# Block sums in the feature stage, values and convolved input kept in high and low parts, and head loads by token halves

## The chip, the cores and the metric

One core of a Trainium2 chip runs the kernel. The metric is the device time in microseconds (us) of one execution, as the median of several runs. A profile of one execution by the hardware profiler stands beside the runs. The engines are named as in the profile: PE (TensorE matmuls) and PEld (its weight loads), DVE (VectorE), ACT (ScalarE), POOL (GpSimd) and SP (SyncE, whose queue issues every DMA of this kernel).

## What is computed

Two layers over 1024 latent tokens of width 1024, with 256 context tokens beside them in the first. The cut below leaves out norms, conditioning and the second layer (a pooling mixer on a grid).

```python
xm, z, og = split(h @ w_in, 3)                    # 3 x 2048 columns
xc = silu(short_conv(xm, conv_w, conv_b))
q, k = headwise(xc, w_q), headwise(xc, w_k)       # 4x4 blocks
v = headwise(xm, w_v)
gates = concat(q, k, v) @ w_gate + b_gate         # two directions
h_f, h_b = mlstm_scan(q, k, v, gates), its mirror # 4 heads of 512
y = sigmoid(og) * headnorm(h_f + h_b) + skip * xc
out = (y * silu(z)) @ w_out
```

The scan is computed by the kernel in its parallel form: for each head and each tile of 128 tokens, scores of the tile's queries against all 1280 tokens, times a matrix of decays, times the values.

## The kernel before, in words

Matmuls take f32r operands. To keep the precision of f32 every operand is split into a high part (a copy by ACT, rounded to f32r) and a low part (the rest, a subtraction by DVE), and a product is three matmuls (`mm3`, L144): high x high, high x low, low x high. All of them are issued at L133. The order of PE's instructions is written out by hand in the stages below; on the other engines the framework orders the work.

**Start (to about 83 us).** Conditioning, norms and `modulate` (L300): the normalized input h, eight tiles of 128 channels by 1024 tokens, in high and low parts that stay in SBUF.

**Feature stage (about 83 to 360 us).** A loop over 16 blocks n of 128 channels. `features(n)` (L342) multiplies a weight tile by h for three token chunks (512, 512, 256), copies the product out (L361 to L364), convolves it, stores the convolved input to `xc_d` (L371, L372) and splits it (L376 to L378). `token_part(n)` (L381) is a generator that runs beside the products of the next block, a step after every second k: for each of ten blocks of 128 tokens it multiplies by `vv` (a block-diagonal matrix for the values and 16 gate columns, in high and low parts) with two matmuls, of 288 and of 144 columns (L398, L399), adds the two halves by a reduction (L400) and collects the values in `vst`, which goes to `v_d` (L402). In passes 2 to 9 POOL adds the high and the low part of h again (L503) and the sum is stored to `h_d` for later.

**Products for z and the output gate (about 360 to 688 us).** The first pair of channel blocks is computed plainly (`plain`, L599), in 64 steps; the generators `gates` (L419: logs of the gates, transposes at L460, scans at L469 to L473, rows stored to `a_d` at L479) and `sums` (L513) are run at given steps of it. `sums(k)` loads two tiles of h from `h_d` (L516), forms four block sums on DVE (L520 to L523) and splits them (L526, L527) into the 16 tiles `T_`. The other seven pairs use Strassen's seven products (`strassen`, L534): sums of weights on POOL (L543 to L546), split at L553 and L554, and the tiles `T_`.

**Heads (about 688 to 1256 us).** Four heads of eight query tiles. A head loads its four tiles of convolved input and one of context (`fetch_x`, L655) and five of values (`fetch_v`, L668), each 512 KB, in f32, and splits them itself (`cast_low`, L649: ACT at L651, then POOL or, in the first head, DVE at L652). `make_A` and `make_q` (L692, L701) make the queries of two tiles at a time. For each tile: `decay` (L736) makes the decay matrix M from gate rows with ACT, and POOL masks the diagonal (L750, L751); `score_chunk` (L713) computes scores for three chunks and multiplies them into M on DVE (L731); `weights` (L753) normalizes M (L757 to L765). One tile later `turn` (L767) transposes M and splits it (L774, L775), and `values` (L778) multiplies by the values; two tiles later `store` (L799) transposes back, scales on DVE (L805), adds on POOL (L806) and stores. A fifth of the second layer's conditioning (`ada_part`, L633) runs on DVE beside the tiles, with weights loaded into `wr`.

**The rest (from about 1256 us)** is the output product, the second layer and its norms.

What orders the work around the change: PE's order by hand; the buffers of a tag (S4: 32 of 4 KB a partition, T5: 5, wr, wh and wl: 2 each, hn: 3, pt: 6; PSUM pa: 3, pb: 2, pc: 3), each free again when its last reader is done; and SP's one queue.

Of the kernel before, what the change touches and what calls it, by code (L numbers as in the profile page):

```python
# [17 lines left out]
P = 128  # L18
# [20 lines left out]
SUM_STEPS = (16, 24, 32, 40)  # L39
# [13 lines left out]
def hybrid_block(ctx: ExitStack, tc: tile.TileContext, xT, ctxT, vecs, w_ada0, w_ada, w_blk, w_krow, blk_mask, w_gate, w_in, b_gate, w_out,  # L53
# [68 lines left out]
    xc_d = dr.tile([KE, P, TA], F32, name="xc_d")  # L122
    v_d = dr.tile([NH, P, 10, DH], F32, name="v_d")
    h_d = dr.tile([KD, P, T], F32, name="h_d")
    y1_d = dr.tile([KE, P, T], F32, name="y1_d")
# [184 lines left out]
    for k in range(KD):  # L310
        if k < 4:
# [4 lines left out]
            modulate(x_sb[k], [(*h[k, hf], slice(512 * hf, 512 * hf + 512)) for hf in range(2)], k, 0)  # L316
        else:
# [3 lines left out]
            modulate(x_sb[k], [(*pair, slice(0, T))], k, 0)  # L321
# [20 lines left out]
    def features(n, side):  # L342
# [28 lines left out]
        nc.sync.dma_start(xc_d[n, :, 0:T], yl)  # L371
        nc.sync.dma_start(xc_d[n, :, T:TA], yc)  # L372
# [3 lines left out]
        for s_, h_, l_ in ((yl, xch[0], xcl[0]), (yc, xch[1], xcl[1])):  # L376
            S.activation(h_, s_, AF.Copy)
            V.tensor_tensor(l_, s_, f(h_), op=ALU.subtract)  # L378
        return xmh, xml, xch, xcl

    def token_part(n, xmh, xml, xch, xcl):  # L381
# [8 lines left out]
        vst = tl("T5", [P, 10, 144])  # L390
        for s in range(10):
            yield
            if s < 8:
                ah, al = xmh[0][:, s * P:(s + 1) * P], xml[0][:, s * P:(s + 1) * P]
            else:
                ah, al = xmh[1][:, (s - 8) * P:(s - 7) * P], xml[1][:, (s - 8) * P:(s - 7) * P]
# [95 lines left out]
    side, parts = iter(()), []  # L492
    with ctx0:
        for n in range(KE):
# [18 lines left out]
        def sums(k):  # L513
            t0, t1 = tl("T5", [P, T]), tl("T5", [P, T])
            for t, kk in ((t0, k), (t1, k + 4)):
                nc.sync.dma_start(t, h_d[kk])  # L516
            b11, b12, b21, b22 = t0[:, :512], t0[:, 512:], t1[:, :512], t1[:, 512:]
            for j in range(1, 5):
                T_[j, k] = tl("S4", [P, 2, 512], F32R)
            V.tensor_tensor(b22, b22, b12, op=ALU.subtract)  # L520
            V.tensor_tensor(b12, b12, b11, op=ALU.subtract)
            V.tensor_tensor(b11, b22, b11, op=ALU.add)
            V.tensor_tensor(b21, b21, b11, op=ALU.subtract)  # L523
            for j, x in ((2, b11), (3, b22), (1, b12), (4, b21)):
                t = T_[j, k]
                S.activation(t[:, 0], x, AF.Copy)  # L526
                V.tensor_tensor(t[:, 1], x, f(t[:, 0]), op=ALU.subtract)  # L527
# [716 lines left out]
```

## Time and profile before

| | |
|---|---|
| median of 3 runs | 2089.25 us (2087.11 to 2090.32) |
| the profiled execution's own time | 2086.98 us |
| its span, first to last instruction | 2085.2 us |
| mean granted clock of PE | 0.979 |
| PE busy | 1994.8 us (96%) |
| DVE busy | 1329.5 us (64%) |
| ACT busy | 772.6 us (37%) |
| POOL busy | 475.4 us (23%) |
| moved by DMA | 272.33 MB, mean 131 GB/s |

A row of the table by stage gives, for a stretch of the span, the busy time of each engine with its number of instructions, the granted clock of PE as a share of full speed, the mean busy share of the 16 DMA engines and what they moved. A row of a timeline begins with the start and the length in us; rows of equal instructions are merged (x3), and a bracket at the end is idle time of the engine before the row, with what ended it. A row of the waits reads: engine, tile and line that waited, <- who ended the wait, total us, times, longest. PE's matmuls overlap, so a row's length holds the latency of its last one; starts give the rate.

### The profile page before, as it was taken

How to read it: one execution, taken by the hardware profiler on the slowest of the kernel's cores; microseconds unless marked ns; L12 is line 12 of the kernel's file. 1: busy time of each engine (PE TensorE's matmuls, PEld its weight loads, DVE VectorE, ACT ScalarE, POOL GpSimd, SP SyncE). 2: the span in 40 equal slices, each digit the busy share in tenths (PEclk: the TensorE clock that was granted, in tenths of full speed). 3: DMA queues.
4: the chain of work that ended last, by engine and by line, in shares of the span. 5: the costliest groups of instructions: out<-in, count | busy, mean ns of one | idle time of the engine just before them, and what ended most of it. 6: DMA issues, size and time to landing. Idle time of an engine off the chain costs nothing.

```text
span 2085.2 us, 26407 instructions
## 1 busy us (share of the span) xinstructions
PE 1994.8 (96%) x10050; PEld 1674.5 (80%) x10050; DVE 1329.5 (64%) x2136; ACT 772.6 (37%) x1201; POOL 475.4 (23%) x482
## 2 busy tenths in 40 slices
PE   7899999799999899999999999999999999999998
PEld 5688888678888787778878888887888888888897
DVE  4877777877767868777677572354657273754444
ACT  5444444333334533333324232443423122224443
POOL 4411100032322313331333211252100000000275
PEclk9999999889999999999999999999999999999999
DMA  7233334444443636135234143434331212224473
GB/s 298 74 130 134 135 104 134 131 147 141 141 152 123 212 116 199 56 130 162 97 114 144 41 152 130 170 140 150 113 121 51 89 58 76 66 94 154 162 256 129
DMA packets 158335, 272.33 MB, mean 131 GB/s; under 512 B 10332, under 2 KB 89692, under 8 KB 158208
## 3 DMA queue, kind: packets, MB, share of 16 engines
q1 hardware_dynamic: 158208, 270.64, 39.1%
q8 instruction: 79, 1.29, 0.3%
q14 instruction: 48, 0.39, 0.1%
HBM read 205.41 MB, written 65.20 MB: 130 GB/s over the span
## 4 chain that ended last, share of the span: by engine, by line
PE 79%; DVE 12%; DMA 3%; issue 3%; POOL 2%; ACT 1%; SPq 0%; DVEq 0%; POOLq 0%; ACTq 0%
PE pa L133 40%; PE pc L133 31%; PE pb L133 6%; PE pb L772 1%; POOL S L961 1%; DMA wr<-in_w_ada_dram 1%; DVE S L306 1%; DVE wl L641 1%; DVE T L763 1%; DVE T L731 1%; POOL hn L941 1%; DVE T L765 1%; DVE S L304 1%; DVE den L759 1%; PE pc L803 1%
## 5 line engine op out<-in xcount | busy, mean ns | idle before, releaser
L133 PE MATMUL pa<-S,wh 128*128 128x512 f32 (+1 forms) x2496 | 723.5, 374 | 7.5 <-DVE S L306 7.2
L133 PEld LDWEIGHTS pa<-S,wh 128*128 128x128 f32 x2496 | 446.1, 190 | 81.3 <-DVE S L306 11.1
L133 PE MATMUL pc<-S,wh 128*128 128x512 f32 (+1 forms) x1616 | 454.9, 367 | 9.3 <-ACT wh L553 6.3
L133 PE MATMUL pa<-S,wl 128*128 128x512 f32 (+1 forms) x1248 | 460.6, 369 | 3.3 <-DVE wl L141 3.3
L133 PEld LDWEIGHTS pc<-S,wh 128*128 128x128 f32 x1616 | 294.6, 190 | 60.0 <-ACT wh L553 6.7
L141 DVE TENSOR_TENSOR wl<-wr,wh 128x1024 fp32r<-128x1024 f32 (+1 forms) x124 | 147.4, 1189 | 271.2 <-ACT wh L139 270.3
L133 PE MATMUL pc<-S,wl 128*128 128x512 f32 (+1 forms) x808 | 295.2, 367 | 3.9 <-DVE wl L554 2.9
L139 ACT ACTIVATE wh<-wr 128x1024 fp32r<-128x1024 f32 (+1 forms) x124 | 124.6, 1005 | 404.7 <-PE pa L133 183.4
L133 PEld LDWEIGHTS pa<-S,wl 128*128 128x128 f32 x1248 | 236.6, 190 | 44.2 <-DVE wl L141 3.7
L133 PE MATMUL pa<-S,S 128*128 128x512 f32 (+1 forms) x1152 | 251.1, 367 | 14.6 <-DVE T L731 14.6
L133 PE MATMUL pc<-S,pt 128*128 128x512 f32 x960 | 233.7, 397 | 0.0
L133 PEld LDWEIGHTS pa<-S,S 128*128 128x128 f32 x1152 | 195.7, 194 | 46.0 <-issue 11.6
L133 PEld LDWEIGHTS pc<-S,pt 128*128 128x128 f32 x960 | 179.5, 190 | 36.0
L133 PEld LDWEIGHTS pc<-S,wl 128*128 128x128 f32 x808 | 153.6, 190 | 29.9 <-DVE wl L554 3.6
L941 POOL TENSOR_TENSOR hn<-hn,pt 128x512 f32<-128x512 f32 (+1 forms) x48 | 77.5, 1615 | 300.7 <-ACT pt L940 290.3
L774 ACT ACTIVATE pt<-pb 128x512 fp32r<-128x512 f32 (+1 forms) x96 | 48.7, 522 | 176.1 <-PE pb L772 134.7
L400 DVE TENSOR_REDUCE T<-pb 128x144 f32<-128x288 f32 x160 | 72.1, 454 | 59.9 <-PE pb L133 59.6
L731 DVE SCALAR_TENSOR_TENSOR T<-pa,T 128x256 f32<-128x256 f32 (+3 forms) x184 | 76.5, 454 | 35.8 <-PE pa L133 30.4
L652 POOL TENSOR_TENSOR S<-S,S 128x1024 fp32r<-128x1024 f32 x35 | 89.3, 2569 | 41.6 <-ACT S L651 41.6
L553 ACT ACTIVATE wh<-T 128x512 fp32r<-128x512 f32 x70 | 42.4, 625 | 100.9 <-POOL T L546 56.7
L775 DVE TENSOR_TENSOR pt<-pb,pt 128x512 fp32r<-128x512 f32 (+1 forms) x96 | 56.5, 596 | 35.2 <-ACT pt L774 34.5
L133 PE MATMUL pb<-S,wh 128*128 128x512 f32 x256 | 78.8, 389 | 0.0
(322 smaller groups left out, 2511.5 us busy)
## 6 DMA issues: line engine op xcount, KB each, us to landing
wr<-in_bw_in_dram SPq DMA_DIRECT2D x40, 512.0 KB, 3.5
wr<-in_w_in_dram SPq DMA_DIRECT2D x34, 512.0 KB, 3.8
S<-xc_d SPq DMA_DIRECT2D x34, 512.0 KB, 5.2
wr<-in_w_ada_dram SPq DMA_DIRECT2D x32, 512.0 KB, 3.9
wr<-in_w_out_dram SPq DMA_DIRECT2D x32, 512.0 KB, 3.5
T<-in_bw_out_dram SPq DMA_DIRECT2D x32, 512.0 KB, 4.4
S<-y_d SPq DMA_DIRECT2D x28, 512.0 KB, 7.3
v_d<-T SPq DMA_DIRECT2D x16, 640.0 KB, 3.9
```

The lines of the kernel that those rows point to most:

```text
L133: PE.matmul(out, lhsT, rhs, start=start, stop=stop)
L139: S.activation(h, r, AF.Copy)
L141: V.tensor_tensor(l, r, f(h), op=ALU.subtract)
L304: V.tensor_scalar(src, src, sc, sh, op0=ALU.mult, op1=ALU.add)
L306: V.tensor_tensor(lo, src[:, c], f(hi), op=ALU.subtract)
L400: V.tensor_reduce(vst[:, s], p.rearrange("p a b -> p b a"), axis=AX.X, op=ALU.add)
L553: S.activation(hi, a, AF.Copy)
L652: eng.tensor_tensor(t, f(t), f(u), op=ALU.subtract)
L731: V.scalar_tensor_tensor(W[:, lo + sh:hi + sh], p[:, lo - o:hi - o], 1.0, W[:, lo + sh:hi + sh], op0=ALU.mult, op1=ALU.mult, accum_out=dp[ ...
L774: S.activation(th[:, :n], p[:, :n], AF.Copy)
L775: V.tensor_tensor(tl_[:, :n], p[:, :n], f(th[:, :n]), op=ALU.subtract)
L941: G.tensor_tensor(acc, acc, sq, op=ALU.add)
```

## The change

- `modulate` stores the modulated input itself to `h_d`, for the latent tokens, in the start stage; the additions of L503 and their stores go.
- `sums` becomes a generator `block_sums`, of which the feature stage runs two steps in each pass from pass 2 on: it loads two tiles, forms the four block sums, and splits and stores one of them a step, to `t_d`. In the plain products the 16 tiles `T_` are loaded from there (`load_sums`), one at every third step from step 12, in the order T2, T3, T1, T4.
- In Strassen's order the product a12 x b21 comes second instead of fourth.
- The convolved input goes to DRAM three times: in f32 (latent tokens only) to `xc_d`, its high part to `xh_d` and its low part to `xl_d`.
- `token_part` uses three matmuls of 144 columns a token block, three blocks to a PSUM bank; ACT copies out the high part, DVE makes the low part and adds the gate columns; the values go to `vh_d` and `vl_d`.
- The heads load both parts, in two token halves and the context, and split nothing. The first half of the next head is loaded in tile 3, its matrix A is made in tile 6 and its first queries in tile 7; there also its gate rows, second half, context and three of its five pairs of value tiles are loaded, the last two pairs in its own tile 0.
- The addition in `store` moves from POOL to DVE.

```diff
-SUM_STEPS = (16, 24, 32, 40)
+T_ORDER = (2, 3, 1, 4)
...
-    def modulate(src, parts, k, j):
+    def modulate(src, parts, k, j, dst=None):
...
         V.tensor_scalar(src, src, sc, sh, op0=ALU.mult, op1=ALU.add)
+        if dst is not None:
+            nc.sync.dma_start(dst, src)
...
-        nc.sync.dma_start(xc_d[n, :, 0:T], yl)
-        nc.sync.dma_start(xc_d[n, :, T:TA], yc)
+        nc.sync.dma_start(xc_d[n], yl)
...
+        for t, dst in ((xch, xh_d), (xcl, xl_d)):
+            nc.sync.dma_start(dst[n, :, 0:T], f(t[0]))
+            nc.sync.dma_start(dst[n, :, T:TA], f(t[1]))
...
-        vst = tl("T5", [P, 10, 144])
...
-            p = pt_("pb", [P, 2, 144])
-            mm(p.rearrange("p a b -> p (a b)"), ah, vv.rearrange("p a b -> p (a b)"), True, False)
-            mm(p[:, 0], al, vv[:, 0], False, True)
-            V.tensor_reduce(vst[:, s], p.rearrange("p a b -> p b a"), axis=AX.X, op=ALU.add)
-        V.tensor_tensor(pre, pre, vst[:, :, P:], op=ALU.add)
-        nc.sync.dma_start(v_d[n // 4, :, :, (n % 4) * P:(n % 4 + 1) * P], vst[:, :, :P])
+        vh, vl = tl("T5", [P, 10, P], F32R), tl("T5", [P, 10, P], F32R)
+        for s0, s1 in ((0, 3), (3, 6), (6, 9), (9, 10)):
+            p = pt_("pb", [P, 3, 144])
...
+                mm3(p[:, s - s0], ah, al, vv[:, 0], vv[:, 1], True, True)
+            q = p[:, :s1 - s0]
+            S.activation(vh[:, s0:s1], q[:, :, :P], AF.Copy)
+            V.tensor_tensor(vl[:, s0:s1], q[:, :, :P], f(vh[:, s0:s1]), op=ALU.subtract)
+            V.tensor_tensor(pre[:, s0:s1], pre[:, s0:s1], q[:, :, P:], op=ALU.add)
+        for t, dst in ((vh, vh_d), (vl, vl_d)):
+            nc.sync.dma_start(dst[n // 4, :, :, (n % 4) * P:(n % 4 + 1) * P], f(t))
...
+    def block_sums():
+        for k in range(4):
+            t0, t1 = tl("S4", [P, T]), tl("S4", [P, T])
+            for t, kk in ((t0, k), (t1, k + 4)):
+                nc.sync.dma_start(t, h_d[kk])
...
+            V.tensor_tensor(b22, b22, b12, op=ALU.subtract)
+            V.tensor_tensor(b12, b12, b11, op=ALU.subtract)
+            V.tensor_tensor(b11, b22, b11, op=ALU.add)
+            V.tensor_tensor(b21, b21, b11, op=ALU.subtract)
+            yield
+            for j, x in ((2, b11), (3, b22), (1, b12), (4, b21)):
+                t = tl("S4", [P, 2, 512], F32R)
+                S.activation(t[:, 0], x, AF.Copy)
+                V.tensor_tensor(t[:, 1], x, f(t[:, 0]), op=ALU.subtract)
+                nc.sync.dma_start(t_d[j - 1, k], f(t))
+                yield
...
-            if 2 <= n < 2 + KD:
-                hs = tl("S4", [P, T])
-                for hf in range(2):
-                    G.tensor_tensor(hs[:, hf * 512:hf * 512 + 512], f(h[n - 2, hf][0]), f(h[n - 2, hf][1]), op=ALU.add)
-                nc.sync.dma_start(h_d[n - 2], hs)
+            if n >= 2:
+                for _ in range(2):
+                    next(sums, None)
...
-            u2 = plus(product("pc", s2, tpart(2)), p1)
-            u3 = plus(product("pa", s3, tpart(3)), u2)
-            done(0, 0, plus(product("pc", a12, b21), p1, p1))
+            done(0, 0, plus(product("pc", a12, b21), p1))
+            u2 = plus(product("pa", s2, tpart(2)), p1, p1)
+            u3 = plus(product("pc", s3, tpart(3)), u2)
...
-                        if count in SUM_STEPS:
-                            sums(SUM_STEPS.index(count))
+                        if count >= GATE_STEPS[0] and count % 3 == 0 and len(T_) < 16:
+                            load_sums(len(T_))
...
-        G.tensor_tensor(ht, ht, ab[1], op=ALU.add)
+        V.tensor_tensor(ht, ht, ab[1], op=ALU.add)
...
-                cast_x(hd, G if h else V)
-                cur = dict(h=h, hd=hd, A=make_A(h))
-                cur["q"] = make_q(hd, cur["A"], 0)
-                cur["R"], cur["rc"] = load_gates(h), rc
...
-            if ti == 7 and h + 1 < NH:
-                rc = load_ctx_gates(h + 1)
-            if ti == 0:
-                fetch_v(hd, h)
+            if ti == 7 and more:
+                nxt["rc"], nxt["R"] = load_ctx_gates(h + 1), load_gates(h + 1)
...
-        if st and ti == 1:
-            cast_v(hd, G)
+            elif more:
+                nxt["q"] = next_q(nxt, 0)
...
-            if ti == 3 and h + 1 < NH:
-                nxt = fetch_x(h + 1)
+            if more and ti == 3:
+                nxt = start_head(h + 1)
+            if more and ti == 6:
+                nxt["A"] = make_A(h + 1)
+            if more and ti == 7:
+                finish_x(nxt)
+                fetch_v(nxt["hd"], h + 1, 0, 3)
...
+        if st and ti == 0 and h:
+            fetch_v(cur["hd"], h, 3, 5)
```

`start_head` loads the first half (`fetch_x(hd, h, 0)`: four tiles of 512 KB), `finish_x` the second half and the context (six tiles). For the first head the order is: first half, A, queries, gate rows, second half and context, all ten value tiles.

## Rows read from the trace of the kernel before

**Rows 1.** The page: busy us, share and instructions of each engine.

```profile
PE 1994.8 (96%) x10050; PEld 1674.5 (80%) x10050; DVE 1329.5 (64%) x2136; ACT 772.6 (37%) x1201; POOL 475.4 (23%) x482
```

**Rows 2.** By stage: busy us of five engines, granted clock, DMA share, GB/s.

```profile
207.00:259.80 52.80, 52.80 (x297) 45.12 (x296) 37.34 (x70) 22.96 (x36) 5.55 (x13) 1.00 0.40 136
...
363.00:383.00 20.00, 14.57 (x61) 10.45 (x60) 18.27 (x39) 9.35 (x18) 0.00 (x0) 0.76 0.32 112
...
411.20:428.40 17.20, 8.02 (x20) 5.52 (x19) 13.98 (x17) 7.86 (x13) 9.19 (x6) 0.60 0.51 143
...
1005.00:1147.00 142.00, 133.80 (x704) 114.21 (x704) 100.45 (x233) 51.23 (x89) 46.22 (x51) 0.98 0.39 125
```

**Rows 3.** Waits of PE in the head stage: total, times, longest.

```profile
PE pa L133 <- DVE T L731: 14.6, 4, 3.7
PE pb L772 <- ACT T L762: 7.4, 3, 3.0
PE pb L772 <- DVE pt L775: 6.9, 4, 2.5
PE pb L772 <- DVE mod L158: 4.7, 2, 2.5
```

**Rows 4.** Timeline of DVE in the first head and at the second head's start.

```profile
798.84 1.28 DVE L641 SCALAR_TENSOR_TENSOR wl<-wr,csil,wl 128x1024 f32<-128x1024 f32 x1 [1.50 <-DMA wr<-in_w_ada_dram]
...
855.18 2.76 DVE L763 TENSOR_SCALAR T<-T,den 128x1152 f32<-128x1152 f32 x1
...
866.00 0.75 DVE L763 TENSOR_SCALAR T<-T,den 128x1024 f32<-128x1024 f32 x1
```

**Rows 5.** Timeline of POOL at the second head's start.

```profile
857.28 7.78 POOL L652 TENSOR_TENSOR S<-S,S 128x1024 fp32r<-128x1024 f32 x3
```

**Rows 6.** Groups by line and shape: count, busy us, mean ns, idle before.

```profile
L652 POOL TENSOR_TENSOR S<-S,S 128x1024 fp32r<-128x1024 f32 x35 | 89.3, 2569 | 41.6 <-ACT S L651 41.6
...
L400 DVE TENSOR_REDUCE T<-pb 128x144 f32<-128x288 f32 x160 | 72.1, 454 | 59.9 <-PE pb L133 59.6
```

**Rows 7.** Timeline of PE in one pass and in a tile; line L772 alone.

```profile
339.71 0.39 PE L133 MATMUL pa<-S,wl 128*128 128x512 f32 x1
...
340.63 0.36 PE L133 MATMUL pb<-vv,S 128*128 128x288 f32 x2
...
341.34 0.39 PE L133 MATMUL pa<-S,wl 128*128 128x512 f32 x1
...
771.61 2.88 PE L133 MATMUL pa<-S,S 128*128 128x512 f32 x12
774.34 1.03 PE L772 MATMUL pb<-ident,T 128*128 128x128 f32 x8
...
L772 PE MATMUL pb<-ident,T x320: 270/272/421, 712.4 to 1257.3; 128*128 128x128 f32 x160
```

**Rows 8.** Waits of PE over the span.

```profile
PE pc L133 <- ACT wh L553: 6.3, 1, 6.3
...
PE pb L460 <- DVE T L453: 3.7, 1, 3.7
...
PE pc L133 <- DVE wl L554: 2.9, 1, 2.9
```

**Rows 9.** Timeline of DVE and ACT where the first seven-product pair begins.

```profile
410.63 0.69 DVE L520 TENSOR_TENSOR T<-T,T 128x512 f32<-128x512 f32 x1 [3.13 <-DMA T<-h_d]
...
414.37 5.10 DVE L527 TENSOR_TENSOR S<-T,S 128x512 fp32r<-128x512 f32 x3
...
417.27 1.15 ACT L553 ACTIVATE wh<-T 128x512 fp32r<-128x512 f32 x2 [0.36 <-POOL T L544]
```

**Rows 10.** DMA issues: count, KB each, median us from issue to landing.

```profile
v_d<-T SPq DMA_DIRECT2D x16, 640.0 KB, 3.9
S<-v_d SPq DMA_DIRECT2D x20, 512.0 KB, 8.7
...
S<-a_d SPq DMA_DIRECT2D x8, 512.0 KB, 6.4
```

More of the change, by code (lines that the diff above doesn't have):

```diff
@@ L120, in vc @@
         return vec[:, o:o + n] if i is None else vec[:, o + i:o + i + w]
-    xc_d = dr.tile([KE, P, TA], F32, name="xc_d")
-    v_d = dr.tile([NH, P, 10, DH], F32, name="v_d")
+    xc_d = dr.tile([KE, P, T], F32, name="xc_d")
+    xh_d = dr.tile([KE, P, TA], F32, name="xh_d")
+    xl_d = dr.tile([KE, P, TA], F32, name="xl_d")
+    vh_d = dr.tile([NH, P, 10, DH], F32, name="vh_d")
+    vl_d = dr.tile([NH, P, 10, DH], F32, name="vl_d")
     h_d = dr.tile([KD, P, T], F32, name="h_d")
+    t_d = dr.tile([4, 4, P, 2, 512], F32, name="t_d")
     y1_d = dr.tile([KE, P, T], F32, name="y1_d")
@@ L315, in hybrid_block @@
                 h[k, hf] = tuple(t[:, k % 2] for t in quad[hf])
-            modulate(x_sb[k], [(*h[k, hf], slice(512 * hf, 512 * hf + 512)) for hf in range(2)], k, 0)
+            modulate(x_sb[k], [(*h[k, hf], slice(512 * hf, 512 * hf + 512)) for hf in range(2)], k, 0, h_d[k])
         else:
@@ L320, in hybrid_block @@
                 h[k, hf] = tuple(t[:, 512 * hf:512 * hf + 512] for t in pair)
-            modulate(x_sb[k], [(*pair, slice(0, T))], k, 0)
+            modulate(x_sb[k], [(*pair, slice(0, T))], k, 0, h_d[k])
     hch = [tl("S4", [P, 4, TC], F32R) for _ in range(2)]
@@ L490, in gates @@
         S.activation(emt, p, AF.Exp, scale=-1.0)
-    side, parts = iter(()), []
+    def block_sums():
[3 more added lines that the diff above has]
+                nc.sync.dma_start(t, h_d[kk])
+            b11, b12, b21, b22 = t0[:, :512], t0[:, 512:], t1[:, :512], t1[:, 512:]
+            V.tensor_tensor(b22, b22, b12, op=ALU.subtract)
[8 more added lines that the diff above has]
+                nc.sync.dma_start(t_d[j - 1, k], f(t))
+                yield
+    side, parts, sums = iter(()), [], block_sums()
     with ctx0:
@@ L511, in hybrid_block, with load_sums @@
         T_ = {}
[L513 to L527, printed above, removed]
+        def load_sums(i):
+            j, k = T_ORDER[i // 4], i % 4
+            T_[j, k] = tl("S4", [P, 2, 512], F32R)
+            nc.sync.dma_start(f(T_[j, k]), t_d[j - 1, k])
         def tpart(j):
@@ L811, in hybrid_block, with start_head, next_q, finish_x @@
     XB = tl("T5", [P, 3, P + TC])
-    rc = load_ctx_gates(0)
     seq = [(h, ti) for h in range(NH) for ti in range(8)]
-    cur = {}
-    nxt = fetch_x(0)
-    st_prev = st_now = None
+    def start_head(h):
+        hd = {}
+        fetch_x(hd, h, 0)
+        return dict(h=h, hd=hd)
+    def next_q(cur, tp):
+        return make_q(cur["hd"], cur["A"], tp)
+    def finish_x(cur):
+        for ci in (1, 2):
+            fetch_x(cur["hd"], cur["h"], ci)
+    cur = start_head(0)
+    cur["A"] = make_A(0)
+    cur["q"] = next_q(cur, 0)
+    cur["rc"], cur["R"] = load_ctx_gates(0), load_gates(0)
+    finish_x(cur)
+    fetch_v(cur["hd"], 0, 0, 5)
+    st_prev = st_now = nxt = None
     for i in range(len(seq) + 1):
@@ L840, in hybrid_block @@
             turn(st_now, 2)
-        if st and ti % 2 and ti < 7:
-            cur["q"] = make_q(hd, cur["A"], (ti + 1) // 2)
-        if st and ti == 1:
-            cast_v(hd, G)
+        if st and ti % 2:
+            if ti < 7:
+                cur["q"] = next_q(cur, (ti + 1) // 2)
+            elif more:
+                nxt["q"] = next_q(nxt, 0)
         if st_prev:
@@ L858, in hybrid_block @@
             next(ada)
+        if st and ti == 7:
+            cur = nxt
         st_prev, st_now = st_now, st
```

67 lines of the change are left out of this document (30 added, 37 removed).

## The prediction

> **What bounds the kernel.** I read the page first. PE is busy for 1994.8 us of a span of 2085.2 [rows 1], so only what shortens PE's own work or closes one of its gaps moves the time. The table by stage then says where the gaps are: none worth a term in the feature stage (52.80 us of 52.80), 5.4 us in the gate part of the first plain products (14.57 busy of 20.00), 9.2 us where the first seven-product pair begins (8.02 of 17.20, at 0.60 of the clock), and 8.2 us in the whole of the third head (133.80 of 142.00) [rows 2]. The reader is to see that the stages are unlike: the change adds PE work in a stage that has no gap and removes side work in those that have some.
>
> The waits of the head stage name who ends them: DVE's score products L731 (14.6 us in four waits), ACT's weights L762, DVE's lows L775 and the conditioning sum L158 [rows 3]. The timeline of a head start tells why DVE is late. L763 over 1152 columns took 2.76 us at 855.18, while POOL was at its casts; at 866.00, with POOL free, 1024 columns took 0.75 [rows 4]. Over the same stretch POOL ran three casts of L652 back to back, 7.78 us from 857.28 [rows 5]; the masks of the next tile stand behind them in POOL's order. 35 such casts took 89.3 us [rows 6]. So the casts hurt twice: they stretch DVE's operations and they hold back POOL's masks.
>
> **Part 1: values in high and low parts (token_part), more PE work.** Per token block the pair of matmuls (288 and 144 columns) becomes three of 144, 160 times. Between two low-weight matmuls at 339.71 and 341.34 lie six matmuls of 512 and one pair: 1.63 us; a 512 takes 0.227 (twelve from 771.61 to 774.34, 2.73 us), so the pair takes 1.63 - 6 x 0.227 = 0.27 [rows 7]. What a 144 costs between its likes no row shows. Nearest are the transposes, 128 columns behind a weight load each: eight busy for 1.03 us, of which 0.27 is the last one's own length, so 0.109 apart [rows 7]. If columns alone counted, 144 would take 0.227 x 144/512 = 0.064 and the triple 0.19, less than the pair. I take two spacings of 0.109 and, for the third, what the pair leaves for its 144: 0.27 less the 288's columns, 0.227 x 288/512 = 0.128, so 0.14. The triple is 0.36, 0.085 more than the pair, and the term 160 x 0.085 = **+13.6 us**; a pass of the stage grows from 17.5 to 18.4. Ends: 3 x 0.14 gives +24; columns alone (the same 432 in both) give 0, with an extra issue at most +2.
> The Trainium skill, "TensorE: Matmul & The Clock Gate", section "Back-to-back issue gap", gives some 81 ns for a sustained matmul of 128 columns; by it the triple would be 0.24 (an estimate) and the term about -4. The spacing of 0.109 in the trace speaks against it, though for transposes of plain f32.
>
> DVE loses ten reductions of 0.45 per pass [rows 6] and gains four lows and four small adds (about 2.8) and its share of the block sums, 0.4 x 8 operations at 0.69 [rows 9], about 2.2. It stays at some 12.9 of 18.4 us (12.4 of 17.5 now, from 37.34 in 52.80 [rows 2]). ACT gains four copies and 0.4 x 4 casts and stays under 11. Cost nothing, hidden by PE; if DVE's cover went, the eviction of the three score banks would stop PE. The additions of hs on POOL (L503) go, worth nothing there.
>
> **Part 2: block sums made early.** sums() leaves the plain stage. There it put four operations of 0.69 and four lows on DVE, four casts on ACT and two loads on SP, four times over. The first set stands inside the gate chain, before L453, for which PE waits 3.7; the last waited for its loads (3.13 at 410.63), its lows stretched over 5.10 us, and the cast of the first sum of weights came only at 417.27 [rows 8, 9]. That is the 6.3 + 2.9 us of wait at the first seven-product pair [rows 8]. Afterwards only the sixteen loads of T remain, and the second product needs nothing from POOL, which gives the sums of weights 2.7 us more.
> Gate part: 5.4 us idle and 0.24 of the clock over 20 us, about 9 with the slow matmuls; I take **-7**, since the transposes there still wait for their own evictions. First pair: 17.20 us for 20 matmuls that need 4.5, so 13 at most; I take **-10**, as the loads of weights now stand among those of T on SP. Ends: 0 and -9, 0 and -13.
> What it adds sits on SP's queue in the feature stage: eight stores of h (before the first pass, DMA share low there), and from pass 2 to 11 two steps of the generator a pass.
>
> **Part 3: heads load both parts.** POOL's 35 casts, DVE's 5 and ACT's 40 go. In the head stage the four waits come to 33.6 us [rows 3]. Not the casts' doing: 3.5 at the first head (its gate rows, L688; 14.6 less three of 3.7), 3.0 in the last tile (the longest of L762), some 3 of L775's in the first head, where DVE itself waited for conditioning weights [rows 4]. That leaves 24, and the matmuls at half clock that follow a wait: PEclk 0.98 over 142 us is up to 2.8 us in the third head [rows 2], and the two beside it are alike; half of the 8 is taken, because PE idles in part of it. Ends 0 and -32; I take **-26** of the 28, near the full amount, since the row that explains the stall (POOL, 7.78) disappears whole.
> The add of store moves from POOL to DVE: 32 x 0.69 = 22 us, in a stage where DVE has 40 us free a head (100.45 of 142.00 [rows 2]). Hidden; without that cover it would delay weights by 0.7 a tile.
> Loads double to 20 tiles of 512 KB a head. At a head's end twelve tiles, two broadcasts and the gate blocks stand on SP. By the slots, the second token half lands some 8 us ahead of its scores. First head: gate rows now stand beside ten tiles of values, where they already took 6.4 to land [rows 10]. I put **+2** for all four starts; ends -3 (the first head's own wait gone) and +20 (5 us each).
>
> **Sum.** 13.6 - 7 - 10 - 26 + 2 = -27.4. The profiled execution took 2086.98 (span 2085.2 and 1.8 around it), the median of three runs is 2089.25, 2.3 above it. Carried over: 2089.25 - 27.4, about **2062**.
>
> **Rivals.**
> *The feature stage waits for its stores (slower).* Per pass there are now w 512, xc 640, v 640 and h 512 KB, 136 GB/s at a DMA share of 0.40 [rows 2]. Afterwards: w 512, xc 512, two parts of 640 each for the convolved input and for the values, and 0.4 x 3072 for the sums: 4813 KB, 4.93 MB. In 18.4 us that is 268 GB/s, at the same efficiency a share of 0.79, at that of the first pair (143 GB/s for 0.51) 0.96 [rows 2]: below one, hence not my forecast, but all of it in one queue. The place is tag T5: xp, y, both value parts and the next xp fill its five buffers, so the next value parts wait until the last ones' stores have landed; ACT stands, the two pb banks stay full, and PE stops at the seventh token block, some 9 us into the pass. From there it decides: such a store takes 3.9 us to land now, value loads under load 8.7 [rows 10]. At 13 us each of passes 2 to 11 loses 4: 2062 + 40 = 2102.
> *The waits come back as waits for loads.* All four head starts wait 5 us for the second half or the gate blocks (DVE stands behind L805, PE behind DVE), the triple is at 3 x 0.14: 2062 + 18 + 10 = 2090, no gain. For it: twelve loads behind the last scores; against it: order and slots above.
> *Short matmuls cost their columns.* Then part 1 is 0: 2062 - 14 = 2048. With the full gaps closed as well (3, 2 and 5 more): 2038. The spacing of 0.109 [rows 7] is against it, if transposes stand for these matmuls.
> The rule of the Trainium skill named in part 1 ("TensorE: Matmul & The Clock Gate") would lead to this case; the trace as far as it goes does not bear it out.
> *It doesn't do what it says*: DVE's delay is not POOL's. Then part 3 gives nothing: 2062 + 26 = 2088. The pair 2.76 and 0.75 [rows 4] speaks plainly against it.
>
> **How the numbers follow.** Forecast 0.60 (its own range 2047 to 2077); columns alone and full gaps 0.16; the feature stage waits for its stores 0.10; waits for loads 0.09; no contention 0.05. Leaving out the slow rival and a sliver below, the range is 2036 to 2086. A measurement tells some 0.2% from no change, 4 us: faster takes the forecast, the short matmuls and a part of the waits for loads: 0.80. The rest of those two cases that give no gain: 0.08; slower 0.12.
>
> **What would show it.** Right: no gap over 1 us at 411, the pass of the feature stage 17.5 grown to about 18.4, no POOL group over 1 us in the heads, L763 never over 1.1 us, PE without a gap of 3.7 at three head starts. Wrong: a pass over 19 us with PE waiting for pb (the first rival); PE waiting at head starts for DVE behind ab or for S<-xh_d (the second); a pass still at 17.5 (the third); L763 still over 2 us (the fourth). The other stages (seven-product pairs, layer B) should keep their times within 2 us.

## The result and the profile after

The changed kernel takes **2062.29 us** (median of 4 runs, 2060.88 to 2064.82); the kernel before took 2088.63 on the same chip (median of 4, 2087.11 to 2090.32). The ratio is 0.9875, with a 95% interval of 0.9858 to 0.9892: 26 us less. The profiled execution took 2061.71, with a span of 2059.9 against 2085.2. The forecast was 2062, so the sum came out. Its terms did not, as the stages show.

The page of the kernel after, to be held against [rows 1]:

```profile
PE 1993.8 (97%) x10210; PEld 1680.1 (82%) x10210; DVE 1244.8 (60%) x2115; ACT 760.5 (37%) x1225; POOL 325.9 (16%) x399
```

PE has 160 matmuls more and is as busy as before, POOL has lost a third of its work, and the span is 25.3 shorter. Where that lies is read from five stretches cut at the same events in both kernels: the first matmul with `vv`, the first gate transpose, the first query matmul of the heads, the first transpose of M, the last one, and the end. The stretches of the kernel before (start and end, length, busy time of PE, PEld, DVE, ACT and POOL, granted clock, DMA share, GB/s):

```profile
98.40:361.60 263.20, 262.97 (x1464) 222.22 (x1462) 191.41 (x355) 111.99 (x162) 24.12 (x58) 1.00 0.38 125
361.60:688.50 326.90, 312.29 (x1371) 255.77 (x1371) 250.61 (x363) 123.34 (x207) 82.13 (x56) 0.96 0.46 145
688.50:712.40 23.90, 20.29 (x99) 17.10 (x98) 14.97 (x33) 16.91 (x29) 7.85 (x11) 0.86 0.75 270
712.40:1257.30 544.90, 513.51 (x2702) 437.16 (x2701) 391.40 (x914) 190.80 (x330) 164.54 (x181) 0.98 0.37 120
1257.30:2085.20 827.90, 809.68 (x3959) 685.48 (x3957) 415.91 (x399) 281.34 (x387) 151.30 (x127) 0.99 0.36 123
```

The same stretches of the kernel after:

```profile
98.60:389.00 290.40, 282.31 (x1624) 240.39 (x1622) 179.04 (x339) 147.09 (x242) 3.87 (x42) 0.98 0.69 237
389.00:694.90 305.90, 305.02 (x1371) 251.79 (x1371) 227.19 (x328) 109.00 (x186) 86.23 (x56) 1.00 0.52 170
694.90:728.10 33.20, 23.52 (x114) 19.19 (x113) 16.62 (x49) 13.86 (x26) 2.55 (x10) 0.85 1.01 353
728.10:1231.10 503.00, 497.36 (x2690) 426.91 (x2689) 340.45 (x927) 160.99 (x297) 39.76 (x115) 1.00 0.49 161
1231.10:2059.90 828.80, 809.24 (x3956) 685.05 (x3954) 416.45 (x400) 281.29 (x387) 148.25 (x126) 0.99 0.37 123
```

The differences are +27.2 in the feature stage, -21.0 in the products for z and the gate, +9.3 at the first head's start, -41.9 in the heads, +0.9 in the rest. The count of matmuls has to be read beside the length: at the first head's start 99 became 114 and in the heads 2702 became 2690, so about a dozen matmuls (some 3 us of PE, 23.52 against 20.29) only moved over the line between those two. The two together give -32.6, which is the number to use. The forecast had +13.6, -17, +2 and -26.

**Feature stage.** Of the 27.2, 8.1 is idle time (290.40 less 282.31), where the stage before had 0.2. The waits of PE of the kernel after name it:

```profile
PE pa L137 <- DVE pt L370: 6.5, 2, 4.4
PE pb L137 <- ACT S L369: 1.2, 1, 1.2
PE pb L137 <- DVE S L370: 0.4, 1, 0.4
```

L369 and L370 are the copies of a chunk of the feature product into its high and low part; with the last of them PE has its bank back. Why DVE's copy came late the second time is seen on DVE's timeline of the kernel after:

```profile
236.87 0.29 DVE L410 TENSOR_TENSOR T<-pb,T 128x128 fp32r<-128x128 f32 x1
238.91 0.69 DVE L510 TENSOR_TENSOR S<-S,S 128x512 f32<-128x512 f32 x1 [1.74 <-DMA S<-h_d]
...
240.60 1.22 DVE L145 TENSOR_TENSOR wl<-wr,wh 128x1024 fp32r<-128x1024 f32 x1
...
242.34 0.42 DVE L370 TENSOR_TENSOR pt<-pa,pt 128x256 fp32r<-128x256 f32 x1
```

The chain of waits of the same stretch (start, length, what) has the load before it, and PE's timeline the stop behind it:

```profile
231.11 7.78 DMA S<-h_d
```

```profile
242.82 1.22 PE L137 MATMUL pa<-S,wh 128*128 128x512 f32 x2 [4.38 <-DVE pt L370]
```

The reader is to see an order, not a load: DVE is idle for 1.74 us at the first operation of a block sum (L510), because the tile of h lands 7.8 us after its issue, and the eviction that PE needs stands behind it and six other operations (3.4 us from 238.91 to 242.34). The first stop, of 2.1 at 140.8, has no such DMA in it; there the eviction stands behind a split of weights (L145, 1.23 from 138.59) and L510 (0.68), and DVE works without a gap. A stop costs more than its length: over the 4.2 us behind the second one the granted clock is at the lower of the two levels:

```profile
242.80:247.00 4.20, 4.18 (x10) 3.35 (x11) 4.20 (x6) 1.26 (x3) 0.00 (x0) 0.50 0.65 197
```

**The matmuls of part 1.** PE's timeline of the kernel after, in a pass without a stop:

```profile
302.28 0.39 PE L137 MATMUL pa<-S,wl 128*128 128x512 f32 x1
...
303.18 0.45 PE L137 MATMUL pb<-vv,S 128*128 128x144 f32 x3
...
303.97 0.39 PE L137 MATMUL pa<-S,wl 128*128 128x512 f32 x1
```

Between the two low-weight matmuls lie six of 512 and one triple: 1.69 us, so the triple takes 1.69 - 6 x 0.227 = 0.33, 0.06 more than the pair of [rows 7]. Averaged over the whole stage it comes to a little more (E3).

**The products.** The waits of [rows 8] (6.3, 3.7, 2.9) are gone; PE is busy for 305.02 of 305.90 at a clock of 1.00 (0.96 before).

**The first head.** PE waits there for 9.6 us, 3.5 before [rows 3, without its three of 3.7]: for the second token half and for the low part of the first queries (L721).

```profile
PE pa L137 <- DMA S<-xh_d: 5.8, 1, 5.8
PE pa L137 <- DMA S<-xl_d: 1.9, 1, 1.9
PE pa L137 <- DVE S L721: 1.9, 1, 1.9
```

SP's timeline of the kernel after shows when the loads were issued:

```profile
686.40 0.65 SPq L806 DMA_DIRECT2D ab<-ga_d  x1
691.81 0.37 SPq L610 DMA_DIRECT2D ga_d<-hn  x1
...
695.10 0.98 SPq L691 DMA_DIRECT2D hn<-a_d  x2
...
699.91 1.36 SPq L677 DMA_DIRECT2D S<-xh_d  x2
701.52 1.58 SPq L677 DMA_DIRECT2D S<-xl_d  x2
```

SP issues nothing from 687 to 691.8, as the store of the last product (L610) waits for its data; the gate rows come next, and the second half only at 699.9. It lands 9 to 10 us later, while the gate rows, the context and the first values move as well:

```profile
702.00:709.00 7.00, 1.18 (x6) 0.66 (x4) 1.64 (x4) 5.09 (x11) 1.17 (x4) 0.72 1.04 402
```

**The heads.** POOL's 35 casts are gone, and its 32 additions went to DVE (39.76 busy instead of 164.54). The normalization that took up to 2.76 in [rows 4] is now L772 (count, then ns: least, median, most):

```profile
L772 DVE TENSOR_SCALAR T<-T,den x32: 390/654/887, 721.9 to 1223.6; 128x1280 f32<-128x1280 f32 x4, 128x1152 f32<-128x1152 f32 x4, 128x1024 f32<-128x1024 f32 x4, 128x896 f32<-128x896 f32 x4
```

The waits of PE in this stretch, 31.2 us before, come to 5.6. The longest of them:

```profile
PE pb L781 <- ACT T L771: 1.9, 1, 1.9
```

### The profile page after: what moved, and what is told of

The parts are those of the page before. It is cut to its first block, busy times and chain, and to the rows that moved or that the text cites. A ratio compares the mean times of both kernels' runs of the same rounds, so it can differ in the third digit from the quotient of the medians.

```text
span 2059.9 us, 26957 instructions
## 1 busy us (share of the span) xinstructions
PE 1993.8 (97%) x10210; PEld 1680.1 (82%) x10210; DVE 1244.8 (60%) x2115; ACT 760.5 (37%) x1225; POOL 325.9 (16%) x399
## 4 chain that ended last, share of the span: by engine, by line
PE 87%; DVE 3%; DMA 3%; POOL 1%; ACT 1%; issue 1%; SPq 0%; DVEq 0%; ACTq 0%; POOLq 0%
PE pa L137 45%; PE pc L137 33%; PE pb L137 7%; PE pb L781 1%; DMA wr<-in_w_ada_dram 1%; POOL hn L969 1%; PE pc L812 1%; DVE S L901 1%; DVE wl L145 1%; DMA wr<-in_w_in_dram 1%; DMA T<-in_bw_out_dram 0%; DMA S<-xl_d 0%; POOL S L989 0%; DVE wl L658 0%; DMA S<-h_d 0%
## 5 line engine op out<-in xcount | busy, mean ns | idle before, releaser
L137 PEld LDWEIGHTS pa<-S,wh 128*128 128x128 f32 x2496 | 447.4, 191 | 88.6 <-DVE S L312 10.8
L145 DVE TENSOR_TENSOR wl<-wr,wh 128x1024 fp32r<-128x1024 f32 (+1 forms) x124 | 147.5, 1189 | 273.0 <-ACT wh L143 272.1
L137 PE MATMUL pc<-S,pt 128*128 128x512 f32 x960 | 227.4, 391 | 1.5 <-DVE S L721 1.1
L740 DVE SCALAR_TENSOR_TENSOR T<-pa,T 128x256 f32<-128x256 f32 (+3 forms) x184 | 78.2, 454 | 33.5 <-PE pa L137 29.3
L794 DVE BATCH_NORM_STATS2 st<-pc 128x6 f32<-128x512 f32 x32 | 22.4, 699 | 86.4 <-PE pc L137 86.4
L145 DVE TENSOR_TENSOR wl<-T,wh 128x1024 fp32r<-128x1024 f32 x32 | 45.5, 1421 | 47.3 <-ACT wh L143 47.2
L137 PEld LDWEIGHTS pb<-vv,S 128*128 128x128 f32 x384 | 61.6, 190 | 11.8 <-ACT S L369 1.9
```

The costliest lines, as they stand in the source:

```text
L137: PE.matmul(out, lhsT, rhs, start=start, stop=stop)
L145: V.tensor_tensor(l, r, f(h), op=ALU.subtract)
L740: V.scalar_tensor_tensor(W[:, lo + sh:hi + sh], p[:, lo - o:hi - o], 1.0, W[:, lo + sh:hi + sh], op0=ALU.mult, op1=ALU.mult, accum_out=dp[ ...
L794: V.bn_stats(b6, pv)
```

## The experiments

Ratios are against runs of the kernel before on the same chip, with their 95% interval. E1 to E4 shared a chip, so did E5 to E8 and E9 to E11.

### E1: the low parts pass through POOL once more

Every low part that a head loads is rewritten in place by POOL, 40 times 1024 columns, so that POOL has the casts' work back while the rest of the change stays.

```diff
+    def again(t, shape):
+        G.tensor_tensor(t, f(t), zero1[:, :, None].to_broadcast(shape), op=ALU.add)
```

> The changed kernel, but every low part that the heads load (ten tiles of 128x1024 a head) passes once more through POOL, in place, by adding zero: POOL has about the work that the casts gave it, and the loads, the early queries and everything else stay. Theory (POOL's casts slowed DVE and held back the masks): the head stage, 503 us from the first to the last transpose in the changed kernel, goes back to about 540, DVE's L763 shows lengths over 2 us again, and the time is 2095 to 2110. Rival (the gain of the heads comes from the early queries and the early loads): the head stage stays under 510 and the time within 6 us of 2062.

Measured: 2065.98 us, ratio 0.9902 (0.9885 to 0.9919). The theory fails as it was put, and the rival's numbers come true: the heads take 507.0, and the time is 3.7 above the change's. E7 shows that the rival's reason was not the cause all the same. POOL's passes in the heads (line, form, count, busy us, mean ns, idle before), and POOL's timeline at the second head:

```profile
L667 POOL TENSOR_TENSOR S<-S,zero 128x1024 fp32r<-128x1024 f32 x40 | 76.9, 1928 | 28.6 <-DMA S<-xl_d 21.1 <-DMA S<-vl_d 7.3 <-issue 0.2
```

```profile
838.94 1.89 POOL L667 TENSOR_TENSOR S<-S,zero 128x1024 fp32r<-128x1024 f32 x1 [1.32 <-DMA S<-xl_d]
...
841.05 1.89 POOL L667 TENSOR_TENSOR S<-S,zero 128x1024 fp32r<-128x1024 f32 x1
```

These are not the casts of [rows 5]: most wait for their own landing (21.1 and 7.3 us of POOL's idle time), a mask of a tile fits between two (840.79), a pass takes 1.93 and not 2.57, and its second operand is one column repeated. DVE's normalizations exceed 1.2 us three times (longest 2.50), five times before. So 77 us of POOL work alone doesn't make the loss; what kind of work, or when, was still open after this run. The two traces tell more. Of the DVE operations that begin inside a cast of the kernel before, 28 of 126 are over 0.3 us longer than the shortest of their line and shape in E7, by 49 us in all; of those that begin inside a pass of E1, 14 of 99 against E2, by 18 us. Half as many were caught, and each lost 1.3 us instead of 1.7. No operation that reads PSUM is among them in either run.

### E2: the same pass on ACT

```diff
+        S.activation(t, f(t), AF.Copy)
```

> The same pass over the same forty low parts, but as a copy on ACT, which adds 40 x 1.05 = 42 us to ACT and leaves POOL alone. Theory (what hurts is POOL beside DVE): within 8 us of the changed kernel, 2060 to 2070, with no DVE row of L763 over 1.1 us. Rival (what hurts is one more step between the load and its use, on whichever engine): as slow as the pass through POOL, over 2090.

Measured: 2062.83, ratio 0.9885 (0.9869 to 0.99). No cost, and the normalizations stay under 0.89. The page line of E1 and that of E2 give the size of POOL's effect on DVE:

```profile
PE 1997.8 (97%) x10210; PEld 1683.5 (81%) x10210; DVE 1262.0 (61%) x2115; ACT 760.6 (37%) x1225; POOL 402.9 (19%) x439
```

```profile
PE 1996.9 (97%) x10210; PEld 1683.3 (82%) x10210; DVE 1244.3 (60%) x2115; ACT 798.1 (39%) x1265; POOL 328.5 (16%) x399
```

The same 2115 DVE instructions take 17.7 us longer beside POOL's passes than beside ACT's.

### E3: the block sums go back into the plain products

`block_sums` and `load_sums` go, `sums` returns at its four steps; the rest of the change stays.

```diff
-            if n >= 2:
-                for _ in range(2):
-                    next(sums, None)
...
-                        if count >= GATE_STEPS[0] and count % 3 == 0 and len(T_) < 16:
-                            load_sums(len(T_))
+                        if count in SUM_STEPS:
+                            sums(SUM_STEPS.index(count))
```

> The changed kernel with the block sums back in the plain products, as in the kernel before (loads of h there, sums on DVE, no t). Theory (the two stops of PE in the feature stage, 2.2 and 4.5 us at passes 3 and 9 with their slow matmuls, come from DVE standing behind the loads of the block sums): the feature stage ends about 13 us earlier, the gate part and the first seven-product pair give about 17 to 21 us back, so 2064 to 2074. Rival (the stops come from the stores of the value parts holding T5): the stops in the feature stage stay, and the time is 2079 or more.

Measured: 2068.17, ratio 0.9912 (0.9895 to 0.9928), as the theory had it, though the 17 to 21 us that were to come back are 15.8. Its feature stage has no idle time left, and its products have the gate waits back:

```profile
100.78:376.72 275.94, 275.94 (x1624) 236.53 (x1623) 160.34 (x307) 138.66 (x226) 3.88 (x42) 1.00 0.60 203
```

```profile
PE pb L471 <- DVE T L464: 6.8, 1, 6.8
```

This splits the +27.2: without the block sums the stage costs +12.7 (275.9 less 263.2), the triples and little else. The block sums bring the other 14.5, of which 8.1 is idle and 6.4 is slow matmuls (busy 282.31 against 275.94, at a granted clock of 0.98 against 1.00). They save 15.8 in the products (321.7 less 305.9), so these two nearly cancel. The medians are 5.9 apart all the same, with intervals that do not meet. Of the 6.8 between the profiled executions these two stages give 1.3; the rest stands in stages that the edit leaves alone (2.2 in the start, 0.9 at the first head, 3.6 in the heads, -1.2 after them). Whether the edit has a part in that is open: the heads alone go from 500.6 (E2) to 506.3 (E8) between runs of the changed kernel.

### E4: the second half before the gate rows in the first head

```diff
-    cur["rc"], cur["R"] = load_ctx_gates(0), load_gates(0)
...
+    cur["rc"], cur["R"] = load_ctx_gates(0), load_gates(0)
```

> The changed kernel with one line moved: the first head loads its second token half and its context ahead of its gate rows. Theory (the loads of the second half stood on SP's queue behind the gate rows of the context, which wait for a buffer of hn): the wait of 5.8 us for S<-xh_d at the first head goes, the stretch from the first query to the first transpose falls from 33.2 us to about 25, and the time is 2052 to 2057. Rival (buffers or the transfers' rate keep the second half late wherever it is issued, or the gate rows become the late ones): the stretch stays over 31 us and the time within 3 us of 2062.

Measured: 2061.04, ratio 0.9877 (0.9858 to 0.9896): not to be told from the change: the theory's time is missed, and of the rival the time holds but not the stretch of over 31. The stretch shrinks from 33.2 to 29.3, but nine matmuls fewer lie in it. The waits of PE in it come to 7.8 against 9.6: those for the second half fall from 7.7 to 4.5 (2.9 and 1.6), 2.1 is the low part of the queries as before (1.9), and 1.2 is new, for scores whose gate rows now come late (L740). The heads behind it take 506.2, 3.2 more. The DMA share of the stretch is 1.01 in both runs; that the transfers' rate, and not their order, is the limit there would fit this but was not tested by itself.

### E5: the block sums from the parts of h in SBUF

The stores and loads of `h_d` go; POOL adds the high and the low part of h, which stay in SBUF, and DVE's part is unchanged.

```diff
-                nc.sync.dma_start(t, h_d[kk])
+                for hf in range(2):
+                    G.tensor_tensor(t[:, 512 * hf:512 * hf + 512], f(h[kk, hf][0]), f(h[kk, hf][1]), op=ALU.add)
```

> The changed kernel, but the block sums take h from its two parts in SBUF (16 additions of 128x512 on POOL, as the kernel before made them) and h is neither stored nor loaded. Theory (PE stops in the feature stage because DVE stands behind the loads of h): from the first product with vv to the first gate transpose 290.4 us become 276 to 280, the two stops go, and the time is 2047 to 2053. Rival (DVE has too much to do there, or POOL's additions slow it as the casts did): the stops stay or move, the stretch is over 286 us and the time over 2058.

Measured: 2052.16, ratio 0.9835 (0.982 to 0.9849): 10 us better than the change by the medians, 8 by the ratios, whose intervals are apart. The feature stage:

```profile
98.60:378.00 279.40, 276.65 (x1624) 236.56 (x1622) 184.35 (x339) 146.96 (x242) 24.44 (x58) 1.00 0.67 232
```

It is 11.0 shorter, at the same number of matmuls: 5.3 of idle time and 5.7 of slow matmuls. The stop of 4.4 is gone, that of 2.1, which had no DMA in it, stays. The products keep their 305.9. So it was the landing in DVE's order, and not DVE's work, that cost most of the 14.5; the rest, 3.5, is left with the same work in the same order.

### E6: E5 and E4 together

> The sums from SBUF and the first head's second half ahead of its gate rows, together. If the two are independent, their gains add: 1 to 2 us below the run with the sums from SBUF alone, 2046 to 2052. If the first head is bound by the transfers there, no difference that can be told.

Measured: 2050.85, ratio 0.9828 (0.9814 to 0.9843). Not to be told from E5.

### E7: only the casts, from POOL to DVE

Two words in the kernel before, nothing else of the change.

```diff
-                cast_x(hd, G if h else V)
+                cast_x(hd, V)
...
-            cast_v(hd, G)
+            cast_v(hd, V)
```

> The kernel before with one thing changed: the 35 subtractions of its casts run on DVE instead of POOL (35 x 1.22 = 43 us more for DVE in the heads). Theory (bursts of POOL's casts hold DVE's operations and POOL's masks at the head starts): the head stage, 544.9 us between the first and the last transpose, falls to 505 to 525, no length of L763 over 1.2 us, and the time is 2050 to 2070. Rival (the heads gained by loading finished parts and by early queries, and POOL was incidental): the head stage stays over 538 and the time is within 6 us of 2088 or above it.

Measured: 2056.89, ratio 0.9851 (0.9832 to 0.9871). Two words take 30 us, as much as the whole change. The stretch of the heads by engine, DVE's casts over the span, and PE's waits in the heads:

```profile
712.50:1225.90 513.40, 504.90 (x2703) 431.69 (x2702) 367.19 (x944) 189.38 (x328) 84.37 (x147) 0.99 0.40 127
```

```profile
L652 DVE TENSOR_TENSOR S<-S,S x40: 1205/1214/1644, 676.1 to 1118.4; 128x1024 fp32r<-128x1024 f32 x40
```

```profile
PE pb L772 <- DVE pt L775: 4.1, 6, 1.0
PE pb L772 <- ACT T L762: 3.0, 1, 3.0
```

The heads fall by 31.5 at the same number of matmuls, the other stages don't move. PE's waits there fall from 31.2 to 8.1: the score products (L731, 11.1 of this stretch) and the conditioning sum (L158, 4.7) are gone, L762 falls by 4.4 and L775 by 2.8. DVE took on 35 casts, 42.5 us at 1.214, and became less busy, 1305.3 against 1329.5 [rows 1]: the casts on POOL had stretched DVE's other operations by 24.2 + 42.5 = 66.7 us. Forty passes in E1 stretched them by 17.7. That is why E1 lost so little, and it settles that the casts on POOL were the cause. Which of E1's differences (one operand repeated, spaced by landings, a mask between) made its passes meet fewer of DVE's operations was not separated.

The prediction named two ways in which the casts hurt, longer DVE operations and late masks. The kernel before shows the first at the stop of the second head's start; DVE, POOL and PE there:

```profile
858.19 2.15 DVE L764 SCALAR_TENSOR_TENSOR T<-T,den,T 128x128 f32<-128x128 f32 x1
860.26 2.56 DVE L765 SCALAR_TENSOR_TENSOR T<-T,den,T 128x256 f32<-128x256 f32 x1
862.74 0.41 DVE L731 SCALAR_TENSOR_TENSOR T<-pa,T 128x256 f32<-128x256 f32 x1
...
867.06 0.48 DVE L765 SCALAR_TENSOR_TENSOR T<-T,den,T 128x256 f32<-128x256 f32 x1
```

```profile
854.87 2.40 POOL L652 TENSOR_TENSOR S<-S,S 128x1024 fp32r<-128x1024 f32 x1
...
865.02 0.29 POOL L751 TENSOR_SCALAR_AFFINE_SELECT T<-T 128x128 f32<-128x128 f32 x1
```

```profile
863.87 0.93 PE L133 MATMUL pa<-S,S 128*128 128x512 f32 x3 [3.69 <-DVE T L731]
```

DVE has no gap there. L763 (2.76 [rows 4]), L764 and L765 take 7.5 us beside four casts, where they take 0.75, 0.35 and 0.48 with POOL free, and the score products that give PE its bank back stand behind them. The masks come at 865.02, after PE has gone on. The stops of 3.7 at 1007.5 and 1149.5 have the same rows. So the stops came from DVE's longer operations; no late mask ended one of the three.

The Trainium skill, "SBUF — State Buffer", section "🔬 SBUF: two separate sides", says that VectorE and GpSimd share a pair of ports as an exclusive lock: a GpSimd instruction and a VectorE instruction in a 2-port mode, or one with two SBUF inputs against a GpSimd one that reads SBUF, do not run side by side, and whichever starts first keeps the pair for its whole instruction. The rows agree in kind: L764 and L765, with two inputs in SBUF, were stretched, and L731, with one in PSUM, kept its 0.41 beside a cast. So do the sizes: the longest normalization was 2.76 beside casts of 2.57 and 2.50 beside passes of 1.93, against 0.89 with neither: 1.9 and 1.6 more, each less than one POOL instruction. In which mode L763 runs, and the lock itself, no run shows.

### E8: the next head's first queries at its own start

```diff
+            if ti == 0 and h:
+                cur["q"] = next_q(cur, 0)
...
-            elif more:
-                nxt["q"] = next_q(nxt, 0)
```

> The changed kernel with the first queries of a head made at its own start again (three of the four heads). Theory (the early queries are a small part): each of the three starts loses 1 to 2 us in which the scores wait for the queries' parts, so 2065 to 2069. Rival (the early queries are what the heads gained by): the three stops of 3.7 us at head starts come back with their slow matmuls, 2075 or more.

Measured: 2063.62, ratio 0.989 (0.9876 to 0.9905). Below the forecast and not to be told from the change; the early queries are worth a few us at most (heads 506.3 against 503.0, times 1.3 apart).

### E9: the add of store back on POOL

```diff
-        V.tensor_tensor(ht, ht, ab[1], op=ALU.add)
+        G.tensor_tensor(ht, ht, ab[1], op=ALU.add)
```

> The changed kernel with the addition of store back on POOL (32 additions of 128x512). Theory (without the casts POOL is free, and one addition a tile off the chain neither helps nor hurts): within 4 us of 2062, the head stage 500 to 507 us. Rival (the addition on POOL slows DVE as the casts did, and its move is the rest of what the heads gained, 10 us beyond the casts): the head stage 508 to 515, the time 2067 to 2074.

Measured: 2063.49, ratio 0.9885 (0.9871 to 0.9898). No difference: the heads take 498.0, but 24 matmuls fewer lie in them, and with the stretch behind them it is 1332.2 against 1331.8. Where POOL has no casts in the heads, the add may stand on either engine.

### E10 to E12: the parts that paid, in the kernel before

E10 takes the kernel before with values and convolved input in f32 as they were, moves the casts and the add to DVE, and makes the block sums early and from SBUF, as E5 does, with a12 x b21 second. E11 is E10 without the block sums. E12 is E10 with the add left on POOL.

```diff
-                cast_x(hd, G if h else V)
+                cast_x(hd, V)
...
-            cast_v(hd, G)
+            cast_v(hd, V)
...
-        G.tensor_tensor(ht, ht, ab[1], op=ALU.add)
+        V.tensor_tensor(ht, ht, ab[1], op=ALU.add)
...
+            if n >= 2:
+                for _ in range(2):
+                    next(sums, None)
```

> The kernel before with what the runs so far credit and nothing else: casts and the addition of store on DVE, block sums in the feature stage from SBUF with T loaded in the plain products, a12 x b21 second. Values and convolved input stay in f32, so the pair of matmuls a token block and the loads of before stay. Theory (the two stores of high and low parts cost PE 12 us in the feature stage and 9 us at the first head and give nothing that casts on DVE don't give): 2028 to 2038. Rival (with the reductions still there DVE has no room for the block sums in the feature stage, or the casts on DVE and the sums collide): PE stops in the feature stage and the time is over 2045.

> The kernel before with the casts and also the addition of store on DVE. Theory (the casts were the whole of POOL's harm): like the run with the casts alone, 2053 to 2060. Rival (the addition on POOL still costs): the head stage falls from 513 to about 505 and the time to 2045 to 2051.

Measured: E10 2050.19, ratio 0.9818 (0.9805 to 0.9831); E11 2059.15, ratio 0.9864 (0.9851 to 0.9878). E10 misses its forecast: the expectation had added up the savings and left nothing for the feature stage, which takes 8.4 more, and the heads take 516.6, not 513.4. In the feature stage PE stops twice for the same eviction (L364), with no landing in it: DVE works without a gap, and operations of a block sum and a split of weights stand ahead, as E12's rows below show. Whether the 160 reductions that DVE keeps there [rows 6] have a part in it was not separated. E11 against E7 says that DVE gains nothing from the add once it has the casts (518.3 in the heads against 513.4). E12 follows from that:

> The run before the last (sums early from SBUF, casts on DVE), with the addition of store left on POOL as in the kernel before. If the addition on DVE took time there because the casts already fill DVE (the head stage was 516.6 us with both, 513.4 with the casts alone), the head stage falls to about 513 and the time to 2046 to 2049. If that difference was chance, the time stays at 2050.

Measured: **2045.65** (2044.44 to 2046.07), ratio 0.9792 (0.9778 to 0.9805). The intervals of E12 and E10 just touch, 4.5 us apart by the medians. E12 is the fastest of all, 43 us below the kernel before and 17 below the change (by ratio 0.9792 against 0.9875, the intervals apart). That the add makes the difference rests on the heads, one profile of each: 512.8 here and 513.4 in E7 with it on POOL, 516.6 and 518.3 with it on DVE. E12's longest wait of PE in the feature stage, DVE ahead of the second of the two stops in it, and its heads:

```profile
PE pa L133 <- DVE pt L364: 4.8, 2, 2.6
```

```profile
230.25 0.69 DVE L503 TENSOR_TENSOR S<-S,S 128x512 f32<-128x512 f32 x1
230.85 1.22 DVE L141 TENSOR_TENSOR wl<-wr,wh 128x1024 fp32r<-128x1024 f32 x1
...
232.19 0.42 DVE L364 TENSOR_TENSOR pt<-pa,pt 128x256 fp32r<-128x256 f32 x1
```

```profile
703.52:1216.28 512.76, 504.51 (x2701) 431.48 (x2700) 367.19 (x943) 192.15 (x333) 85.50 (x148) 0.99 0.40 126
```

By stage it stands at +9.9, -18.1, -0.6, -32.1 and -0.1 against the kernel before. It keeps the two gains of the change and pays for neither the triples nor the loads of two parts; the +9.9 is what the early block sums still cost.

## Why the prediction was right, and where its steps were not

- **Part 1, +13.6: right.** E3 measures +12.7, 0.079 a triple (forecast 0.085), and a pass of 18.4 (275.9 over 15). The window shown gives 0.06, so the term rests on the whole stage. The rival "short matmuls cost their columns" falls: three of 144 take 0.33, 0.11 each, as the transposes did. The Trainium skill's figure of some 81 ns for 128 columns ("TensorE: Matmul & The Clock Gate", section "Back-to-back issue gap") would have made the triple 0.24 (an estimate), shorter than the pair; the measured 0.33 against 0.27 decides against it here.
- **"Cost nothing, hidden by PE": the step that failed.** The prediction counted DVE's time in a pass (12.9 of 18.4, and there was room: 13.65 of 18.00 in the row below) and not its order. DVE ran its operations in order, and the first operation of a block sum waited for a load that PE's next bank then waited for too: +14.5, of which E5 takes 11.0 away. It named as the danger, should DVE's cover go, the eviction of the three banks, and that is where PE stopped; as a rival it named stores that hold tag T5. That rival fell: no wait for T5 shows, and the stores of the values land in 4.0 and 6.3 us, far from the 13 it needed. Its DMA load was right: in this stretch of the kernel after a share of 0.77 at 268 GB/s, forecast 0.79 at 268.

```profile
280.60:298.60 18.00, 18.00 (x107) 15.40 (x106) 13.65 (x24) 9.94 (x16) 0.15 (x3) 1.00 0.77 268
```

- **Part 2, -7 and -10: too small, measured -21.0.** Each was taken below its end (9 and 13, together 22) to leave a rest of waits, and hardly a rest was left: PE idles 0.9 us in 305.9, and the clock is at 1.00.
- **Part 3, -26: the waits right, the slow clock too small.** E7 gives the casts alone: -31.5. The waits that the prediction put down to them came to 24, and 23.1 went. The rest, 8.4, is matmuls that no longer run behind a stop at the lower clock, of which the prediction had counted half of 8 and then taken a little off. Of its two ways for the casts to hurt, the stops show the longer DVE operations; the late masks ended none of the three long ones.
- **Loads, +2: about right in sum, wrong in its reason.** The first head and the heads together give -32.6, so all but the casts gives -1.1. The first head alone loses some 6 (9.3 less the moved matmuls; its waits are 9.6 against 3.5), by the mechanism of the second rival, in one of the four starts and not in all. The heads behind it gain about 7 beyond the casts; their waits are 5.6 against 8.1 in E7, and E8 puts at most some 3 of it on the early queries. How the rest divides was not separated.
- **The rest, 0:** +0.9.

So the sum came out by luck, as three errors cancelled: 14.5 not seen in the feature stage, against 4 in the products and some 9 in the heads counted too small. What the prediction had right is the cause of the heads' gain and the price of the triples. The rival that DVE's delay is not POOL's falls with E7.

## What to carry to other kernels

Before a change is built that prepares operands in an earlier stage, move the bulk work that disturbs the chain to another engine that has room: two words did here what extra matmuls and twice the loads did. Where an engine frees banks for PE, look at what stands ahead of the freeing operation in its order, and let nothing there wait for a landing: DVE had a quarter of its time free here, and PE stopped for 4.4 us. Taking the data from SBUF helped (E5); work alone ahead of the eviction still cost stops of 2 to 3 us (E5, E10, E12). Check the terms of a sum by stage and by count of instructions, not the total: this total was right with three terms wrong.

## What the runs showed that was not expected

- 35 POOL casts of 89.3 us [rows 6] stretched DVE by 66.7 us, 40 POOL passes of 76.9 us by 17.7. The amount of POOL work does not give the cost; how many of DVE's operations on SBUF meet it does (28 and 14).
- Stops of PE cost more than their length, and not by one factor: 8.1 us idle came with 6.4 of slower matmuls in the feature stage, 23.1 with 8.4 in the heads. The stop of 2.1 that E5 keeps came with none (clock 1.00).
- With many loads standing in SP's queue the core moved 402 GB/s at a share above 1 in the page's measure, and 512 KB took 9.4 to 10.8 us from issue to landing (medians by tensor, at the first head), where the loads of h, of the same size, took 5.5 (median) in the feature stage.
